# A two-layer decoder trunk on one core: the sums of the third modulation pair on VectorE

## The chip, the cores and the metric

The kernel runs on one core of a Trainium2 chip. Its engines work side by side, each through its own queue in order: TensorE (matrix products and transposes into PSUM; PE, with its weight loads as PEld), VectorE (DVE), ScalarE (ACT), GpSimd (POOL) and SyncE (SP), whose queue here issues nearly all large transfers. The metric is the device time of one execution in microseconds.

## The reference, cut to what matters

Two layers. In each, a conditioning vector `c` gives six modulation vectors of 1024 numbers. They shift, scale and gate the two halves of the layer:

```python
cond = jax.nn.silu(c)
mod = cond @ w_mod[l] + b_mod[l]            # w_mod[l]: 1024 x 6144
sh1, sc1, ga1, sh2, sc2, ga2 = split(mod, 6)
h = rms_norm(x, g_norm1[l]) * (1.0 + sc1) + sh1
z = h @ w_in[l]                             # 512 x 1024 by 1024 x 2560
... three token mixers on the parts of z, joined as y ...
x = x + ga1 * (y @ w_out[l])
h = rms_norm(x, g_norm2[l]) * (1.0 + sc2) + sh2
x = x + ga2 * hier_moe(h, ...)              # top-1 group, top-2 of 8 experts
```

All of it is float32. The six vectors are handled as three pairs of 2048 columns of `w_mod`: pair 0 is (sh1, sc1), pair 1 is (ga1, sh2), pair 2 is (sc2, ga2). Pair 2, "the third pair", is first used by the router's preparation (sc2) and by the experts (ga2).

## The kernel before, in words

Memory is an arena of 25 units of 128 x 2048 float32 (1 MiB each). `alloc` takes a free one, by default the one that has been free longest (`alloc(True)` the one freed last). All large weights go through one ordered stream: `want_layer` (L202) sorts the blocks of the input projection (`want_in`, two per chunk) and of pairs 1 and 2 (`want_mod`, eight each) by due step, `pump(keep)` issues blocks from SP as long as more than `keep` units are free, `get` hands one out and `release` frees it. SP is in program order, so a block whose unit is still being read holds up all blocks behind it. The order on the other engines in this stage is made by a planner that lists work by its own estimate of when it is ready.

The input projection of a layer runs as five chunks of 512 columns (`CHUNKS`: keys, queries, queries and keys of the third mixer, values, the rest), each of eight steps j, 40 steps in all (`z_chunk`, L486). A step contracts 128 rows for four tiles of 128 tokens. Each product is made of three (`mm3`, L301: high by high L302, high by low L303, low by high L304), so a step is twelve products of 128x512. The weights are split into a high half by ScalarE (L298) and a low half by GpSimd (L299), one split for every two steps, two buffers deep. After the eighth step the four accumulators (PSUM banks 0 to 3) are copied out, by ScalarE and VectorE in turn (L310, L308); the next chunk reuses the banks.

While a chunk is computed, the chunk before it is normalized and rotated (`rope_work`, L501): per token tile a square (ScalarE L506), a sum (VectorE L507), two small ScalarE steps (L294, L295), three products on VectorE (L512 twice at half width, L514), a sum on GpSimd (L516) and a product on VectorE (L518). TensorE transposes the four tiles at steps 4 to 7 (`heads_T`, L520; L523), and they are copied out again by L308 and L310. That is the work of chunks 1 to 3 beside the projection. Chunk 4 begins the softmax of the first mixer.

The modulation pairs 1 and 2 are computed in the same stage. A unit (`mod_unit`, L242, products at L245) takes one 128x2048 block of `w_mod` and makes four float32 products, side by side in four column tiles, with one column of silu(c), broadcast to 32, as weights; eight units sum in PSUM bank 7. `mods(c)` (L667) is called ahead of each step. With `PLAN[l] = (1, 18)` pair 1 has its units at steps 1, 3, ..., 15 and pair 2 at steps 18, 20, ..., 32. After the eighth, `mod_row` (L256) adds the bias, `mod_spread` (L272) writes the row to memory and reads it back as columns and as a broadcast, and `mod_finish` (L287) prepares the scale four steps later (`LATER`).

After the projection come the mixers, the output projection, the router, and the experts: 32 experts in 16 pairs per layer, with 6 MiB of weights each pair.

Of the kernel before, what the change touches and what calls it, by code (L numbers as in the profile page):

```python
# [18 lines left out]
OP = mybir.AluOpType  # L19
# [16 lines left out]

KA, QA, VA, QK, UV = 512, 0, 1024, 1792, 1536
CHUNKS = (KA, QA, QK, VA, UV)
PLAN = ((1, 18), (1, 18))
LEAD = (3, 3)  # L40
LATER = (4, 4)
ROOM = (0, 2)
# [36 lines left out]
def trunk(ctx: ExitStack, tc: tile.TileContext, I, out, dbg=None):  # L79
    nc = tc.nc  # L80
# [7 lines left out]
    PS = [psump.tile([128, 512], F32, name=f"ps{i}") for i in range(8)]  # L88
# [17 lines left out]
    def alloc(newest=False):  # L106
        return Unit(newest)
# [5 lines left out]
    ones_f = smallp.tile([128, 32], F32, name="ones_f")  # L113
    tok = smallp.tile([128, 2 * NT], F32, name="tok")
    ccol = smallp.tile([128, 8], F32, name="ccol")
    csil = smallp.tile([128, 8], F32, name="csil")
# [35 lines left out]
    def issue():  # L152
        key, parts = stream.popleft()
        u = alloc()
        held[key] = u
        for view, src in parts:
            nc.sync.dma_start(view(u.ap), src)

    def pump(keep=0):
        while stream and len(freed) > keep:  # L160
            issue()

    def get(key):
        while key not in held:
            issue()
        return held[key].ap

    def release(key):
        held.pop(key).free()

    def want_mod(l, i, j0=0, j1=8):
        w = I["w_mod"][l].rearrange("(p j) n -> p j n", j=8)
        for j in range(j0, j1):
            want(("mod", l, i, j), lambda a: a, w[:, j, i * 2048:(i + 1) * 2048])
# [10 lines left out]
    def want_out(l):  # L185
        w = I["w_out"][l].rearrange("(k p) n -> p k n", p=128)
        for h in range(4):
            want(("out", l, h), lambda a: a.rearrange("p (k n) -> p k n", k=2), w[:, 2 * h:2 * h + 2, :])
# [13 lines left out]
    def want_layer(l):  # L202
        if l == 0:
            want_mod(0, 0)
        g1, g2 = PLAN[l]
        need = [(8 * n + 4 * h - 2 - LEAD[l], want_in, (l, c, h)) for n, c in enumerate(CHUNKS) for h in range(2)]
        need += [(g + 2 * j, want_mod, (l, i, j, j + 1)) for i, g in ((1, g1), (2, g2)) for j in range(8)]
        for _, f, args in sorted(need, key=lambda x: x[0]):
            f(*args)
        if l + 1 < L:  # L210
            want_mod(l + 1, 0)
        want_out(l)
        for pr in range(16):
            want_pair(l, pr)
# [8 lines left out]
    for l in range(L):  # L223
        want_layer(l)
# [17 lines left out]
    def mod_unit(l, i, j, bank):  # L242
        w = get(("mod", l, i, j))
        for g in range(4):
            nc.tensor.matmul(PS[bank][32 * g:32 * g + 32, :], csil[:, j:j + 1].to_broadcast([128, 32]), w[:, g * 512:(g + 1) * 512],  # L245
                             start=j == 0, stop=j == 7, tile_position=(0, 32 * g))
        release(("mod", l, i, j))

    def mod_bias(l, i, bm, q=None):
        nc.vector.memset(bm, 0.0)  # L250
# [4 lines left out]
    def mod_row(bank, bm):  # L255
        nc.vector.tensor_tensor(mrow, PS[bank], bm, op=OP.add)  # L256
# [15 lines left out]
    def mod_spread(i):  # L272

        row = mod_d[i:i + 1, :]
        nc.sync.dma_start(row.rearrange("o (g n) -> (o g) n", g=4), mrow[0:128:32, :])
        col = lambda h: row[:, D * h:D * h + D].rearrange("o (p j) -> (o p) j", j=8)
        if i == 0:
            nc.sync.dma_start(cols[:, SH1, :], col(0))
            nc.sync.dma_start(cols[:, 6, :], col(1))
        elif i == 1:  # L280
            nc.sync.dma_start(cols[:, SH2, :], col(1))
            nc.sync.dma_start(ga1_of[0], row[:, 0:D].to_broadcast([128, D]))
        else:
            nc.sync.dma_start(cols[:, 6, :], col(0))
            nc.sync.dma_start(ga2, row[:, D:2 * D].to_broadcast([128, D]))

    def mod_finish(i):  # L287
        if i == 0:
            scaled(SC1, cols[:, 6, :], G1)
        if i == 2:  # L290
            scaled(SC2, cols[:, 6, :], G2)
# [29 lines left out]
    def front(l):  # L321
# [13 lines left out]
        W = [wk[i // 4].ap[:, 512 * (i % 4):512 * (i % 4) + 512] for i in range(16)]  # L335
# [3 lines left out]
        rpu = alloc()  # L339
        tab = rpu.ap.rearrange("p (n a m d) -> p n a m d", n=4, a=2, m=NT)  # L340
        hu = [alloc() for _ in range(4)]
# [102 lines left out]
        keep = [ROOM[l]]  # L444
# [36 lines left out]
        keep[0] = 1  # L481
        pump(keep[0])

        unit = [0]

        def z_chunk(done, each=None):  # L486
# [178 lines left out]


        def mods(c):  # L667
            g1, g2 = PLAN[l]

            def f(j):  # L670
                for i, g in ((1, g1), (2, g2)):
                    k, odd = divmod(8 * c + j - g, 2)
                    if 0 <= k < 8 and not odd:
                        mod_unit(l, i, k, 7)
                        pump(keep[0])
                        if k == 7:
                            mod_row(7, W[11 + i])
                            mod_spread(i)
                    if 8 * c + j == g + 14 + LATER[l]:
                        mod_finish(i)  # L680
            return f

        def zr(c):
# [70 lines left out]
        z_chunk(uv_done, both(mods(4), early))  # L754
        for k in range(2 * NT):
            nc.sync.dma_start(y_d[l][128 * k:128 * k + 128, :], I["k_zero"])
        for u in (rpu, *hu):
            u.free()
        yau, ycu, ypu, rt = [alloc() for _ in range(2)], alloc(), alloc(), alloc()
        U["yah"], U["yal"] = (u.ap.rearrange("p (h t) -> p h t", h=4) for u in yau)  # L760
# [525 lines left out]
```

## Time and profile before

| | us |
|---|---|
| median of 3 runs | 1162.53 |
| lowest and highest | 1159.25, 1163.12 |
| the profiled execution | 1165.25 |
| its span in the trace | 1163.3 |

Busy time in the profiled execution: TensorE 1053.3 us, its weight loads 573.1, VectorE 568.8, ScalarE 356.8, GpSimd 299.3. The busy time of an engine is a share of the whole; what bounds a stage is read from that stage. A row of a timeline gives start, duration, engine, line, operation, output and input with sizes; in brackets the idle time of the engine in front of it and what ended that.

### The profile page before, as it was taken

The page shows a single profiled execution, that of the slowest core. Times are in us where ns is not written, and L with a number is a line of the kernel's source. Part 1 is how long each engine was busy: PE and PEld are TensorE (multiplying, and loading weights), DVE is VectorE, ACT ScalarE, POOL GpSimd, SP SyncE. Part 2 cuts the span into 40 slices and gives each one's busy share as a digit, 9 for nine tenths or more (in the row PEclk, how much of TensorE's full clock was granted, in tenths as well). Part 3 has the DMA queues.
Part 4 walks back from the last instruction along what each step waited for, and adds up shares of the span by engine and source line. Part 5 has one row for each costly group of instructions (what it writes and reads, how often), then busy time and mean ns, then how long its engine had stood idle before and what let it go on. Part 6 is the DMA issues. An engine that isn't in the chain of part 4 may idle for free. (4 is left out here: it accounts for less than half of the span.)

```text
span 1163.3 us, 14911 instructions
## 1 busy us (share of the span) xinstructions
PE 1053.3 (91%) x5120; PEld 573.1 (49%) x5120; DVE 568.8 (49%) x1293; ACT 356.8 (31%) x900; POOL 299.3 (26%) x262
## 2 busy tenths in 40 slices
PE   5999999999899989989769999999988988999885
PEld 1567766577533323333227676667764333333322
DVE  3577756778622222222294777577775221222227
ACT  2333345564311111111132333556633111111110
POOL 5655531002222221221044555210022211122100
PEclk9899999999899999999979999999999999999998
DMA  9966436726849999999996535540477999999993
GB/s 378 397 222 250 163 116 220 291 72 232 310 140 399 410 390 409 390 375 398 402 317 256 181 127 181 181 133 2 143 291 262 385 409 409 399 399 384 400 396 126
DMA packets 91194, 329.91 MB, mean 284 GB/s; under 512 B 19288, under 2 KB 23576, under 8 KB 76448
## 3 DMA queue, kind: packets, MB, share of 16 engines
q1 hardware_dynamic: 74992, 307.86, 69.4%
q0 software_dynamic: 15184, 18.03, 4.9%
q10 hardware_dynamic: 864, 2.17, 0.5%
q8 instruction: 73, 1.20, 0.4%
q14 instruction: 81, 0.66, 0.2%
HBM read 338.87 MB, written 30.97 MB: 318 GB/s over the span
## 5 line engine op out<-in xcount | busy, mean ns | idle before, releaser
L1117 PE MATMUL ps<-unit,unit 128*64 128x512 f32 x1120 | 272.1, 611 | 19.2 <-DMA unit<-w 16.9
L1117 PEld LDWEIGHTS ps<-unit,unit 128*64 128x64 f32 x1120 | 88.4, 140 | 191.7 <-issue 180.5
L302 PE MATMUL ps<-unit,unit 128*128 128x512 f32 x448 | 182.1, 412 | 0.4 <-ACT unit L298 0.4
L303 PE MATMUL ps<-unit,unit 128*128 128x512 f32 x448 | 177.2, 396 | 2.8 <-POOL unit L299 1.5
L304 PE MATMUL ps<-unit,unit 128*128 128x512 f32 x448 | 176.0, 395 | 0.5 <-DVE unit L299 0.5
L1137 PE MATMUL ps<-unit,unit 128*64 128x512 f32 x560 | 138.1, 615 | 16.4 <-PEq L1185 14.7
L1122 DVE SCALAR_TENSOR_TENSOR unit<-ps,slot_f,unit 128x256 f32<-128x256 f32 x35 | 16.9, 484 | 251.9 <-ACT unit L1121 251.9
L1086 POOL DMA_INDIRECT unit<-xn_d,slot_i x62 | 63.0, 1017 | 285.0 <-PE ps L1097 164.3
L1121 ACT ACTIVATE unit<-ps 128x256 f32<-128x256 f32 x35 | 13.5, 385 | 392.2 <-PE ps L1117 392.2
L299 POOL TENSOR_TENSOR unit<-unit,unit 128x1024 fp32r<-128x1024 f32 (+1 forms) x46 | 104.9, 2284 | 102.0 <-ACT unit L298 102.0
L298 ACT ACTIVATE unit<-unit 128x1024 fp32r<-128x1024 f32 (+1 forms) x92 | 88.0, 963 | 117.1 <-PE ps L304 65.6
L302 PEld LDWEIGHTS ps<-unit,unit 128*128 128x128 f32 x448 | 84.4, 189 | 36.0 <-issue 16.4
L303 PEld LDWEIGHTS ps<-unit,unit 128*128 128x128 f32 x448 | 84.8, 189 | 22.4 <-DVE unit L299 3.5
L304 PEld LDWEIGHTS ps<-unit,unit 128*128 128x128 f32 x448 | 84.1, 188 | 19.2 <-DVE unit L299 1.2
L1151 DVE TENSOR_TENSOR unit<-ps,unit 128x512 f32<-128x512 f32 x62 | 42.9, 692 | 84.6 <-PE ps L1137 84.6
L1137 PEld LDWEIGHTS ps<-unit,unit 128*64 128x64 f32 x560 | 35.8, 137 | 90.5 <-issue 80.5
L534 ACT ACTIVATE unit<-unit,sm 128x512 f32<-128x512 f32 (+3 forms) x96 | 53.3, 556 | 32.9 <-DVE sm L532 32.4
L310 ACT ACTIVATE unit<-ps 128x512 f32<-128x512 f32 (+3 forms) x84 | 40.8, 490 | 72.0 <-PE ps L304 22.9
L1106 DVE TENSOR_SCALAR unit<-ps,cols 128x128 f32<-128x128 f32 x132 | 45.1, 405 | 33.5 <-PE ps L1097 32.6
L1091 POOL DMA_INDIRECT y_d<-unit,slot_y x31 | 31.6, 1020 | 113.4 <-DVEq L1187 46.5
L299 DVE TENSOR_TENSOR unit<-unit,unit 128x1024 fp32r<-128x1024 f32 (+1 forms) x46 | 54.9, 1199 | 11.0 <-ACT unit L298 10.4
L308 DVE COPY unit<-ps 128x512 f32<-128x512 f32 (+3 forms) x80 | 43.9, 553 | 31.8 <-PE ps L523 12.3
(223 smaller groups left out, 1317.0 us busy)
## 6 DMA issues: line engine op xcount, KB each, us to landing
unit<-w SPq DMA_DIRECT2D x256, 512.0 KB
unit<-w SPq DMA_DIRECT2D x64, 1024.0 KB
unit<-w_mod SPq DMA_DIRECT2D x48, 1024.0 KB
unit<-w_in SPq DMA_DIRECT2D x16, 1024.0 KB
y_d<-k_zero SPq DMA_DIRECT2D x16, 512.0 KB
unit<-w_out SPq DMA_DIRECT2D x8, 1024.0 KB
unit<-y_d SPq DMA_DIRECT2D x16, 512.0 KB
unit<-w_in SPq DMA_DIRECT2D x8, 512.0 KB
```

The costliest lines, as they stand in the source:

```text
L298: nc.scalar.activation(hi.bitcast(F32R), src, AF.Copy)
L299: (eng or nc.gpsimd).tensor_tensor(lo.bitcast(F32R), src, hi, op=OP.subtract)
L302: nc.tensor.matmul(o, ahi.bitcast(F32R), bhi.bitcast(F32R), start=first, stop=False)
L303: nc.tensor.matmul(o, ahi.bitcast(F32R), blo.bitcast(F32R), start=False, stop=False)
L304: nc.tensor.matmul(o, alo.bitcast(F32R), bhi.bitcast(F32R), start=False, stop=last)
L308: nc.vector.tensor_copy(dst, src)
L534: nc.scalar.activation(dst[:, :n], dst[:, :n], AF.Exp, bias=mx, scale=-1.0, accum_out=z)
L1086: nc.gpsimd.indirect_dma_start(out=dst, out_offset=None, in_=xn_d, in_offset=bass.IndirectOffsetOnAxis(ap=idx, axis=0), bounds_check=S - 1 ...
L1106: nc.vector.tensor_scalar(dst[:, j, :], p, cols[:, SC2, j:j + 1], cols[:, SH2, j:j + 1], op0=OP.mult, op1=OP.add)
L1117: nc.tensor.matmul(ph[64 * r:64 * r + 64, :], xT[:, j, 64 * r:64 * r + 64], ws[:, j % 4], start=j == 0, stop=j == 7, tile_position=(0, 64 ...
L1137: nc.tensor.matmul(PS[banks[n]][64 * r:64 * r + 64, :], hidT[b][:, j, 64 * r:64 * r + 64], w2[r][:, j, n, :], start=j == 0, stop=j == 1, t ...
L1151: nc.vector.tensor_tensor(ys[b][:, cs], p, ga2[:, cs], op=OP.mult)
```

## The change

Pair 1 stays as it is. Pair 2's eight blocks no longer go through TensorE as they come. VectorE multiplies each block by its column of silu(c), as a scalar per partition, and adds it to a 128 x 2048 accumulator `acc` that takes one unit of the arena until the end of chunk 4. The steps are 2, 6, ..., 30. At step 33 TensorE sums `acc` over the partitions with four products against ones; the bias row, the spread and the finish (step 37) follow as before. The due steps in the stream change alike.

```diff
-PLAN = ((1, 18), (1, 18))
+PLAN = ((1, 2, 33), (1, 2, 33))
...
-        need += [(g + 2 * j, want_mod, (l, i, j, j + 1)) for i, g in ((1, g1), (2, g2)) for j in range(8)]
+        need += [(g + d * j, want_mod, (l, i, j, j + 1)) for i, g, d in ((1, g1, 2), (2, g2, 4)) for j in range(8)]
...
+    def mod_part(l, i, j, acc):
+
+        w = get(("mod", l, i, j))
+        if j == 0:
+            nc.vector.tensor_scalar(acc, w, csil[:, j:j + 1], None, op0=OP.mult)
+        else:
+            nc.vector.scalar_tensor_tensor(acc, w, csil[:, j:j + 1], acc, op0=OP.mult, op1=OP.add)
+        release(("mod", l, i, j))
+
+    def mod_sum(acc, bank):
+        for g in range(4):
+            nc.tensor.matmul(PS[bank][32 * g:32 * g + 32, :], ones_f[:, 0:32], acc[:, g * 512:(g + 1) * 512],
+                             start=True, stop=True, tile_position=(0, 32 * g))
...
         keep[0] = 1
         pump(keep[0])
 
+        acc = alloc(True)
...
             def f(j):
-                for i, g in ((1, g1), (2, g2)):
-                    k, odd = divmod(8 * c + j - g, 2)
-                    if 0 <= k < 8 and not odd:
-                        mod_unit(l, i, k, 7)
-                        pump(keep[0])
-                        if k == 7:
-                            mod_row(7, W[11 + i])
-                            mod_spread(i)
-                    if 8 * c + j == g + 14 + LATER[l]:
-                        mod_finish(i)
+                now = 8 * c + j
+                k, odd = divmod(now - g1, 2)
+                if 0 <= k < 8 and not odd:
+                    mod_unit(l, 1, k, 7)
+                    pump(keep[0])
+                    if k == 7:
+                        mod_row(7, W[12])
+                        mod_spread(1)
+                k, odd = divmod(now - g2, 4)
+                if 0 <= k < 8 and not odd:
+                    mod_part(l, 2, k, acc.ap)
+                    pump(keep[0])
+                if now == e2:
+                    mod_sum(acc.ap, 7)
+                    mod_row(7, W[13])
+                    mod_spread(2)
+                if now == e2 + LATER[l]:
+                    mod_finish(2)
...
-        for u in (rpu, *hu):
+        for u in (acc, rpu, *hu):
             u.free()
```

## Rows read from the trace of the kernel before

**Rows 1.** The page, part 1: busy time, share and instructions of each engine.
```profile
PE 1053.3 (91%) x5120; PEld 573.1 (49%) x5120; DVE 568.8 (49%) x1293; ACT 356.8 (31%) x900; POOL 299.3 (26%) x262
```
**Rows 2.** By stretch, layer 0's chunks and its experts: busy, clock, DMA share, GB/s.
```profile
36.40:66.10 29.70, 29.10 (x128) 19.33 (x129) 12.99 (x16) 10.00 (x15) 20.57 (x15) 0.91 1.02 393
66.10:95.60 29.50, 28.73 (x146) 19.93 (x145) 22.02 (x26) 10.46 (x21) 14.93 (x8) 1.00 0.60 220
95.60:122.80 27.20, 27.20 (x138) 19.72 (x136) 21.37 (x25) 10.58 (x21) 15.04 (x8) 1.00 0.44 152
122.80:151.00 28.20, 28.20 (x145) 19.93 (x144) 21.19 (x25) 9.87 (x22) 14.98 (x8) 1.00 0.54 187
400.00:592.00 192.00, 167.46 (x698) 62.04 (x696) 50.32 (x97) 26.88 (x82) 33.86 (x37) 0.96 1.01 388
```
**Rows 3.** The same view, layer 1's chunks 1 to 3.
```profile
640.00:668.50 28.50, 27.73 (x140) 19.02 (x139) 20.74 (x24) 10.44 (x20) 14.94 (x8) 1.00 0.51 182
668.50:696.00 27.50, 27.50 (x141) 20.14 (x141) 21.89 (x25) 10.54 (x20) 15.03 (x8) 1.00 0.40 137
696.00:725.00 29.00, 29.00 (x149) 20.47 (x148) 22.32 (x27) 10.39 (x21) 14.96 (x8) 1.00 0.54 182
```
**Rows 4.** TensorE's waits in layer 0's projection: total us, times, longest.
```profile
PE ps L303 <- POOL unit L299: 0.8, 1, 0.8
```
**Rows 5.** TensorE's timeline around two modulation units.
```profile
55.74 1.06 PE L245 MATMUL ps<-unit,csil 128*32 128x512 f32 x8
...
61.85 0.39 PE L303 MATMUL ps<-unit,unit 128*128 128x512 f32 x1
62.08 0.39 PE L304 MATMUL ps<-unit,unit 128*128 128x512 f32 x1
62.40 1.06 PE L245 MATMUL ps<-unit,csil 128*32 128x512 f32 x8
63.40 0.50 PE L302 MATMUL ps<-unit,unit 128*128 128x512 f32 x1
```
**Rows 6.** VectorE's groups by form, whole span: total us, mean ns, idle before.
```profile
L1207 DVE TENSOR_TENSOR unit<-unit,unit 128x1024 f32<-128x1024 f32 x16 | 18.9, 1220 | 11.7 <-DMA unit<-y_d 11.6
L567 DVE SCALAR_TENSOR_TENSOR unit<-unit,sm 128x512 f32<-128x512 f32 x8 | 6.0, 752 | 0.3
L567 DVE SCALAR_TENSOR_TENSOR unit<-unit,sm 128x128 f32<-128x128 f32 x8 | 2.8, 352 | 0.2
L641 DVE TENSOR_SCALAR unit<-unit,sm 128x512 f32<-128x512 f32 x8 | 3.8, 487 | 0.0
L641 DVE TENSOR_SCALAR unit<-unit,sm 128x128 f32<-128x128 f32 x8 | 2.1, 284 | 0.1
```
**Rows 7.** VectorE's timeline in chunk 0: its longest idle times.
```profile
55.83 0.15 DVE L393 TENSOR_SCALAR gsub<-gsub 128x1 f32<-128x1 f32 x1 [6.45 <-DMA gsub<-g_sub_a]
65.03 0.43 DVE L512 TENSOR_TENSOR unit<-unit,unit 128x256 f32<-128x256 f32 x1 [9.05 <-ACT unit L310]
```
**Rows 8.** VectorE's timeline in chunk 2.
```profile
96.62 0.75 DVE L512 TENSOR_TENSOR unit<-unit,unit 128x256 f32<-128x256 f32 x2
97.28 2.88 DVE L514 TENSOR_TENSOR unit<-unit,unit 128x512 f32<-128x512 f32 x1
...
101.74 0.68 DVE L518 TENSOR_TENSOR unit<-unit,sm 128x512 f32<-128x512 f32 x1
102.34 0.68 DVE L514 TENSOR_TENSOR unit<-unit,unit 128x512 f32<-128x512 f32 x1
102.94 0.67 DVE L507 TENSOR_REDUCE sm<-unit 128x8 f32<-128x512 f32 x1
...
105.27 2.95 DVE L512 TENSOR_TENSOR unit<-unit,unit 128x256 f32<-128x256 f32 x2
...
113.08 2.86 DVE L518 TENSOR_TENSOR unit<-unit,sm 128x512 f32<-128x512 f32 x1 [1.40 <-ACT unit L310]
115.86 0.68 DVE L308 COPY unit<-ps 128x512 f32<-128x512 f32 x1
```
**Rows 9.** GpSimd's timeline in chunk 2: the splits.
```profile
97.12 2.50 POOL L299 TENSOR_TENSOR unit<-unit,unit 128x1024 fp32r<-128x1024 f32 x1 [4.84 <-ACT unit L298]
...
105.31 2.62 POOL L299 TENSOR_TENSOR unit<-unit,unit 128x1024 fp32r<-128x1024 f32 x1 [0.85 <-ACT unit L298]
...
113.01 2.38 POOL L299 TENSOR_TENSOR unit<-unit,unit 128x1024 fp32r<-128x1024 f32 x1
```
**Rows 10.** GpSimd's groups in chunk 2 (95.6 to 122.8 us).
```profile
L299 POOL TENSOR_TENSOR unit<-unit,unit 128x1024 fp32r<-128x1024 f32 x4 | 9.9, 2476 | 7.0 <-ACT unit L298 7.0
L516 POOL TENSOR_TENSOR unit<-unit,unit 128x512 f32<-128x512 f32 x4 | 5.2, 1293 | 4.8 <-DVE unit L514 4.8
```
**Rows 11.** TensorE's timeline in chunk 2: units and transposes.
```profile
107.91 1.06 PE L245 MATMUL ps<-unit,csil 128*32 128x512 f32 x8
108.91 0.66 PE L523 MATMUL ps<-ident,unit 128*128 128x128 f32 x4
...
119.70 0.60 PE L523 MATMUL ps<-ident,unit 128*128 128x128 f32 x4
```
**Rows 12.** ScalarE's timeline in chunk 2, around a conversion of weights.
```profile
102.45 0.30 ACT L294 ACTIVATE sm<-sm,eps_t 128x8 f32<-128x8 f32 x1 [1.02 <-DVE unit L518]
...
104.19 1.05 ACT L298 ACTIVATE unit<-unit 128x1024 fp32r<-128x1024 f32 x1
```
**Rows 13.** The third pair's finish on VectorE, step 34's first products, the finish's first reader.
```profile
159.92 0.17 DVE L259 SCALAR_TENSOR_TENSOR cols<-cols 128x8 f32<-128x8 f32 x1
160.40 1.13 PE L543 MATMUL ps<-unit,unit 64*128 64x512 f32 x4
L914 DVE TENSOR_TENSOR unit<-unit,cols x2: 173/180/186, 192.7 to 770.7; 128x32 f32<-128x32 f32 x2
```
**Rows 14.** SP's timeline: issues of pair 1's blocks of steps 3 to 9.
```profile
27.54 2.96 SPq L157 DMA_DIRECT2D unit<-w_mod  x2
...
35.75 1.82 SPq L157 DMA_DIRECT2D unit<-w_mod  x2
```
**Rows 15.** GpSimd's splits, whole span: shortest, median and longest in ns.
```profile
L299 POOL TENSOR_TENSOR unit<-unit,unit x46: 1289/2392/2815, 37.3 to 746.1; 128x1024 fp32r<-128x1024 f32 x38, 128x512 fp32r<-128x512 f32 x8
```

More of the change, by code (lines that the diff above doesn't have):

```diff
@@ L204, in want_layer @@
             want_mod(0, 0)
-        g1, g2 = PLAN[l]
+        g1, g2, _ = PLAN[l]
         need = [(8 * n + 4 * h - 2 - LEAD[l], want_in, (l, c, h)) for n, c in enumerate(CHUNKS) for h in range(2)]
-        need += [(g + 2 * j, want_mod, (l, i, j, j + 1)) for i, g in ((1, g1), (2, g2)) for j in range(8)]
+        need += [(g + d * j, want_mod, (l, i, j, j + 1)) for i, g, d in ((1, g1, 2), (2, g2, 4)) for j in range(8)]
         for _, f, args in sorted(need, key=lambda x: x[0]):
@@ L667, in mods @@
         def mods(c):
-            g1, g2 = PLAN[l]
+            g1, g2, e2 = PLAN[l]
             def f(j):
-                for i, g in ((1, g1), (2, g2)):
-                    k, odd = divmod(8 * c + j - g, 2)
-                    if 0 <= k < 8 and not odd:
-                        mod_unit(l, i, k, 7)
-                        pump(keep[0])
-                        if k == 7:
-                            mod_row(7, W[11 + i])
-                            mod_spread(i)
-                    if 8 * c + j == g + 14 + LATER[l]:
-                        mod_finish(i)
+                now = 8 * c + j
[16 more added lines that the diff above has]
+                    mod_finish(2)
             return f
```

## The prediction

> **What bounds the kernel now.** I read the page first: TensorE is busy 91% of the span, VectorE 49%, GpSimd 26% [rows 1]. These are averages, so I went to the stage that the change touches, the input projection: per layer 40 steps in five chunks of eight, of which chunks 0 to 3 matter here. In layer 0 the turns of the chunks lie at about 36, 66.1, 95.6, 122.8 and 151.0 us; layer 1 repeats the picture some 575 us later. In the table by stretch TensorE is busy for all of chunks 2 and 3 and for all but 0.8 us of chunk 1, in both layers, at full clock [rows 2, 3]. The list of TensorE's waits has a single 0.8 us on GpSimd's low half of the weights [rows 4]. So TensorE sets the pace there, and what leaves its queue is worth its pitch, until something else is late. The rest of the text asks what is late next.
>
> **TensorE: what goes.** A modulation unit is four column-tiled products. The product before one starts at 62.08 us, the first after it at 63.40: 1.32 us, where two ordinary products stand 0.23 apart [rows 5]. A unit costs 1.09 us. Per layer eight go (those at steps 18, 20, ..., 32) and one like them comes (the sum over partitions, at step 33). Net seven: 7 x 1.09 = 7.6 us per layer, 15.3 us for both. By place: three before the end of chunk 2 (3.3 us), four before the end of chunk 3 (4.4 us), none in chunk 1; in chunk 4 one leaves and one comes. Were it all, 1165.3 us of the profiled execution would become 1150.0, and the median 1162.5 (2.7 us below that execution) would become 1147.3.
>
> **VectorE: what comes.** No row shows its 128x2048 operation with two inputs in SBUF; the nearest bound it. The same form takes 0.752 us for 512 columns and 0.352 for 128, 1.04 ns per column, so 2.35 us for 2048; 1024 columns of a plain sum take 1.22, twice that is 2.44 [rows 6]. I take 2.35, or 2.3 from start to start. The first step of a layer has one input; 0.487 and 0.284 us at 512 and 128 columns give 1.30 [rows 6]. Per layer 1.3 + 7 x 2.35 = 17.8 us. The steps fall at 2 and 6 of every chunk from 0 to 3: two per chunk.
>
> **Where that lands.** In chunk 0 VectorE is idle for long: 6.45 and 9.05 us in front of two of its instructions [rows 7]. Two steps are free there. Chunks 1 to 3 are another matter. They hold the rope work: per chunk VectorE runs some twenty operations, GpSimd four splits and four sums, and the two disturb each other. A 128x512 product that takes 0.68 us alone takes 2.88 when GpSimd starts a split at about the same time (97.28 against 97.12); the same at 105.27 and 113.08 against 105.31 and 113.01 [rows 8, 9]. So a VectorE operation with two inputs in SBUF stands still for a GpSimd operation, and their times add. The new step is of this kind. The load of chunk 2:
> - GpSimd: 9.9 us of splits and 5.2 of sums, 15.1 us [rows 10].
> - VectorE, undisturbed, start to start: eight half-width operations at 0.34 and eight full ones at 0.60 us, 7.5 us [rows 8].
> - Together 22.6 us which exclude each other. The old length is 27.2; TensorE alone would need 27.2 - 3.3 = 23.9.
> - With two new steps 22.6 + 4.6 = 27.2 us. With one, 24.9.
>
> That is the heart of the forecast: with two steps in a chunk this pair of engines needs as long as the chunk takes today. It is no loose bound, since from the chunk's start to the last rope operation (115.94 us) the pair already works almost without a gap. Chunk 3 is 28.2 us now, its load the same. Something is lost at each turn, where VectorE must first empty the accumulators; I take 0.7 us, below the 0.8 of rows 4 and above nothing.
>
> **Who waits for VectorE.** TensorE transposes the roped tiles at steps 4 to 7. The last at step 7 starts at 119.70, its operand is done at 115.94: 3.8 us of slack, of which the removed units take 3.3 [rows 8, 11]. The accumulators are copied by VectorE too, behind whatever is queued. And ScalarE's conversion of the next weights (104.19) stands in its queue behind a rope instruction that waits for VectorE, so the split behind it ends at 107.93, and its first reader stands some 1 us later [rows 9, 11, 12]. A new step before these places pushes all three.
>
> **Order on VectorE.** It is the planner's, not the program's: the finishing of the third pair, written at step 36, ran at 159.92 us, when TensorE was only about to begin step 34 (160.40) [rows 13]. So a new step may run as soon as its block is in and a gap is planned. The arena lets blocks come some six steps ahead in chunk 1; I expect about one step per layer to move from the later chunks forward to idle time in chunk 0 or at the end of chunk 1, and cannot tell more from the trace.
>
> **The sum, likeliest case, per layer.** Chunk 1: unchanged but for one more wait of the size of rows 4, +0.8. Chunk 2 with two steps: 27.2 + 0.7 = 27.9 against 27.2, +0.7. Chunk 3 with one: 24.9 + 0.7 = 25.6 against 28.2, -2.6. Total -1.1, for two layers -2.2 us: 1163.0 for the profiled execution, 1160.3 on the footing of the median. No part of the 15.3 us is lost on TensorE; it is handed to the other two engines.
>
> **DMA and queues.** The same 48 blocks, each 1 MiB, come in another order: two of the third pair stand ahead of needed ones in chunk 0, where DMA is full at 393 GB/s: 2 x 2.7 = 5.3 us later for the second pair's. Their units at steps 5 and later came from blocks issued 25 us and more before use [rows 5, 14], so I price this at nothing; if that cover were gone it would be up to 5.3 us, once. In chunks 1 to 3 DMA is busy 0.44 to 0.60, which covers one buffer less. SP now waits for VectorE before it reuses a third-pair buffer, with the input weights queued behind; at 137 to 220 GB/s that has room [rows 2, 3]. A new step waits for its block on VectorE, and behind it wait rope work and copies: the blocks come early enough except for that same 5.3. The bias row, the spread and the finish move one step later (2.7 us); the first reader of the result runs 33 us after the finish [rows 13], so nothing. The experts' stage is bound by DMA at 388 GB/s [rows 2], but its stream begins when buffers come free, which moves with the front, so I let gains and losses through in full.
>
> **A rule against the change.** The splits stretch little: 2.39 us in the median, 2.82 at most [rows 15], so by the rows VectorE holds GpSimd up by 0.4 us at most. The Trainium skill (SBUF — State Buffer, Who interferes with whom) says that whichever of the two starts first holds the shared port for its whole instruction and the other blocks fully. No operation of 2.3 us on VectorE meets a split in this trace, so it shows only the one side. By the rows, the sum above stands; by the rule, a split meeting a new step ends up to 2.3 us late, and the split behind which TensorE stands is already just in time. That is the slow rival below.
>
> **Rivals.**
> 1. **Splits held (slower).** A new step starts just ahead of a split and holds it; TensorE stands for it, and the roped tiles come late. For it: the chain of rows 8, 9 and 12 has 1 us of slack. Against: the planner may put steps elsewhere. Per layer: chunk 1 one step on the chain, +2.35; chunk 2 the rope ends 20.3 + 4.7 = 25.0 us in, then a transpose (0.44) and a step (2.73), 28.2, +1.0; chunk 3 the same 28.2, 0. Together +3.4, two layers +7: 1169.3. With a further 2.35 in chunks 2 and 3 it is +16, 1178. It decides when both steps of a chunk run before its last rope operation.
> 2. **More hoisting (faster).** Two steps or more leave chunks 2 and 3 for idle time. Chunks 2 and 3 at 25.6 each: -1.6 - 2.6 = -4.2 per layer, -8.4: 1154.1.
> 3. **All hidden.** The full 15.3 us: 1147.3. Against it: 23.9 us for TensorE is less than 24.9 for the pair with even one step.
> 4. **The order undone.** The planner bunches steps late, ahead of the softmax of chunk 4: about rival 1's time, and counted there.
>
> **How the numbers follow.** A measurement can tell about 0.3%, 3.5 us, from no change. Chances: likeliest (1159 to 1166) 0.40; rival 1 0.27; rival 2 0.25; rival 3 0.08. Faster is 2 and 3, 0.33; same 0.40; slower 0.27. The range goes from 1150, which leaves out rival 3 and a corner of 2, to 1174, which leaves out the upper half of rival 1; together under 0.2. The likeliest case's own range is 1157 to 1166.
>
> **What would show it.** Right: 16 of 48 units gone from TensorE (eight records each, so 128 of 384) and two new sums over partitions, 16 new VectorE operations of 2.3 us, some stretched by GpSimd; chunk 2 as long as before and chunk 3 shorter; new idle time of TensorE on GpSimd's split, on VectorE's rope results and on its copies, of several us per layer. Wrong: TensorE gapless with chunks 2 and 3 under 25 us (rivals 2, 3), or splits later by 2 us with chunk 1 longer by over 2 (rival 1), or new steps waiting for DMA.

## The result and the profile after

The changed kernel takes 1178.17 us in the median of four runs (1175.88 to 1178.80), the kernel before 1162.82 beside it. The ratio is 1.0124 with a 95% interval of 1.0098 to 1.0149: slower by 14.4 us, above the top of the range (1174). The profiled execution is the fastest of the four, 1175.88 us with a span of 1174.0, against 1165.25 and 1163.3. One execution on record, the profiled one of e1 below, was far slower than all others of its kernel (5101.77 us) and enters no figure.

The page, part 1, answers [rows 1]: TensorE lost 11.3 us of busy time, VectorE gained 43.8.

```profile
PE 1042.0 (89%) x5008; PEld 576.6 (49%) x5008; DVE 612.6 (52%) x1309; ACT 355.7 (30%) x900; POOL 314.1 (27%) x262
```

The new operation, all its records in both layers (shortest, median, longest in ns, first and last start):

```profile
L255 DVE SCALAR_TENSOR_TENSOR unit<-unit,csil,unit x14: 2337/2344/4477, 56.9 to 725.5; 128x2048 f32<-128x2048 f32 x14
```

By stretch, from turn to turn (a turn is ScalarE's first rope square of the next chunk; the last stretch ends at the first softmax operation); columns as in [rows 2]. First layer 0's chunks 1, 2 and 3, then layer 1's:

```profile
64.49:94.03 29.54, 28.78 (x146) 19.89 (x145) 25.89 (x27) 10.43 (x21) 17.43 (x8) 1.00 0.68 254
94.03:124.78 30.75, 27.18 (x122) 20.51 (x121) 27.98 (x28) 10.20 (x21) 15.40 (x8) 0.94 0.55 195
124.78:160.69 35.91, 28.69 (x124) 22.38 (x122) 27.41 (x30) 12.14 (x24) 16.96 (x8) 0.90 0.26 88
647.51:677.08 29.57, 28.65 (x146) 19.91 (x145) 27.65 (x27) 10.53 (x21) 17.66 (x8) 1.00 0.57 213
677.08:708.38 31.30, 26.41 (x114) 20.39 (x113) 25.29 (x27) 10.32 (x20) 17.02 (x8) 0.95 0.38 131
708.38:741.53 33.15, 28.18 (x124) 21.98 (x122) 25.14 (x29) 12.14 (x24) 16.95 (x8) 0.95 0.29 96
```

With the same ends the kernel before has 29.45, 27.18 and 31.84 us in both layers, at a clock of 1.00. So chunk 1 is unchanged, chunk 2 grew by 3.6 and 4.1 us, chunk 3 by 4.1 and 1.3: 13.1 us, nearly the whole loss. TensorE has seven units fewer in these two stretches of layer 0 and eight fewer in layer 1 (in layer 0 pair 1's last unit came later and fell into chunk 2, at 95.59 us): 15 x 1.09 = 16.4 us less to do. So some 29.5 us of new delay came in.

TensorE's waits (total us, times, longest) in layer 0's projection, which answer [rows 4], then in layer 1's:

```profile
PE ps L538 <- DVE unit L322: 7.8, 2, 6.7
PE ps L317 <- POOL unit L313: 2.8, 3, 1.5
...
PE ps L538 <- DVE unit L322: 5.5, 2, 4.4
...
PE ps L317 <- POOL unit L313: 3.4, 3, 1.9
PE ps L316 <- DVE unit L322: 1.9, 1, 1.9
```

L538 is the transpose of a roped tile, L322 VectorE's copy out of PSUM, L313 the split. Where the single wait was 0.8 us, waits from turn to softmax are now 3.6 + 7.2 us in layer 0's chunks 2 and 3 and 4.9 + 5.0 in layer 1's (length less TensorE's busy time). About 9 us more are in no list of waits. Most of it is the clock: in each of these four stretches TensorE did some 3 to 4.5 us of its work at half clock, 14.5 us in all by the granted clock in slices of 1 us. Half of that is lost, an estimated 7 us.

How it comes about is seen in chunk 2 of layer 0. VectorE's timeline, the counterpart of [rows 8]:

```profile
109.96 2.34 DVE L255 SCALAR_TENSOR_TENSOR unit<-unit,csil,unit 128x2048 f32<-128x2048 f32 x1
112.23 0.68 DVE L533 TENSOR_TENSOR unit<-unit,sm 128x512 f32<-128x512 f32 x1
...
114.89 2.82 DVE L533 TENSOR_TENSOR unit<-unit,sm 128x512 f32<-128x512 f32 x1 [1.38 <-POOL unit L531]
117.64 4.46 DVE L255 SCALAR_TENSOR_TENSOR unit<-unit,csil,unit 128x2048 f32<-128x2048 f32 x1
122.02 0.68 DVE L322 COPY unit<-ps 128x512 f32<-128x512 f32 x1
```

ScalarE, GpSimd and TensorE in the same stretch:

```profile
112.94 0.30 ACT L308 ACTIVATE sm<-sm,eps_t 128x8 f32<-128x8 f32 x1 [7.46 <-DVE unit L533]
113.15 1.04 ACT L312 ACTIVATE unit<-unit 128x1024 fp32r<-128x1024 f32 x1
...
114.81 5.14 POOL L313 TENSOR_TENSOR unit<-unit,unit 128x1024 fp32r<-128x1024 f32 x2
...
114.82 0.66 PE L538 MATMUL ps<-ident,unit 128*128 128x128 f32 x4 [0.89 <-ACT unit L324]
115.23 0.47 PE L316 MATMUL ps<-unit,unit 128*128 128x512 f32 x1
117.22 0.50 PE L317 MATMUL ps<-unit,unit 128*128 128x512 f32 x1 [1.51 <-POOL unit L313]
...
118.53 0.63 PE L318 MATMUL ps<-unit,unit 128*128 128x512 f32 x1
118.96 0.63 PE L316 MATMUL ps<-unit,unit 128*128 128x512 f32 x1
...
122.76 0.66 PE L538 MATMUL ps<-ident,unit 128*128 128x128 f32 x4 [1.17 <-DVE unit L322]
```

Read it in two chains. The first step, at 109.96, pushes the rope product at 112.23. ScalarE waits for that product, and the conversion of the next weights stands in its queue behind it (113.15); the split follows at 114.81, where it was 113.01 in [rows 9], and TensorE stands 1.51 us for it. The second step, at 117.64, begins beside a running split and takes 4.46 us. Behind it stands the copy of tile 1 out of a PSUM bank (122.02, where [rows 8] has 115.86), and tile 3's transpose needs that bank: 122.76, where [rows 11] has 119.70. From 118.1 to about 121.2 products follow one another in 0.43 us, not 0.23: TensorE's second level, 1.2 GHz.

Chunk 3 of layer 0 has the same two chains, and the longer wait. VectorE, GpSimd and TensorE:

```profile
141.88 2.34 DVE L255 SCALAR_TENSOR_TENSOR unit<-unit,csil,unit 128x2048 f32<-128x2048 f32 x1
145.37 2.81 DVE L533 TENSOR_TENSOR unit<-unit,sm 128x512 f32<-128x512 f32 x1 [1.15 <-POOL unit L531]
148.11 2.34 DVE L255 SCALAR_TENSOR_TENSOR unit<-unit,csil,unit 128x2048 f32<-128x2048 f32 x1
150.37 0.74 DVE L322 COPY unit<-ps 128x256 f32<-128x256 f32 x2
...
142.03 3.30 POOL L531 TENSOR_TENSOR unit<-unit,unit 128x512 f32<-128x512 f32 x1 [1.57 <-DVE unit L529]
145.30 2.33 POOL L313 TENSOR_TENSOR unit<-unit,unit 128x1024 fp32r<-128x1024 f32 x1
...
136.89 0.60 PE L538 MATMUL ps<-ident,unit 128*128 128x128 f32 x4
...
150.93 1.09 PE L538 MATMUL ps<-ident,unit 128*128 128x128 f32 x4 [6.68 <-DVE unit L322]
```

The first step holds GpSimd's rope sum (3.30 us; before, all 24 of these sums took 1.29 to 1.31). The last rope product then waits, and is itself stretched by the split that begins beside it; the second step goes ahead of the copies. Tile 0 was transposed at 136.89 and could have been copied from 137.5 on; its copy by VectorE runs at 150.37, and the third transpose of the chunk, tile 2's, which uses tile 0's bank, waits 6.68 us for it.

Chunk 2 of layer 1 went another way. There both steps, at 678.94 and 696.32, run ahead of the last rope product (702.81). The second one holds a split, and TensorE stands for that split. VectorE, GpSimd and TensorE:

```profile
696.32 2.35 DVE L255 SCALAR_TENSOR_TENSOR unit<-unit,csil,unit 128x2048 f32<-128x2048 f32 x1
...
697.67 3.20 POOL L313 TENSOR_TENSOR unit<-unit,unit 128x1024 fp32r<-128x1024 f32 x1 [2.33 <-ACT unit L312]
...
700.92 0.50 PE L317 MATMUL ps<-unit,unit 128*128 128x512 f32 x1 [1.90 <-POOL unit L313]
```

### The profile page after: what moved, and what is told of

It reads as the page before. It is cut to its first block, busy times and chain, and to the rows that moved or that the text cites. A ratio compares the mean times of both kernels' runs of the same rounds, so it can differ in the third digit from the quotient of the medians.

```text
span 1174.0 us, 14726 instructions
## 1 busy us (share of the span) xinstructions
PE 1042.0 (89%) x5008; PEld 576.6 (49%) x5008; DVE 612.6 (52%) x1309; ACT 355.7 (30%) x900; POOL 314.1 (27%) x262
## 5 line engine op out<-in xcount | busy, mean ns | idle before, releaser
L317 PE MATMUL ps<-unit,unit 128*128 128x512 f32 x448 | 180.9, 404 | 7.4 <-POOL unit L313 6.2
L316 PE MATMUL ps<-unit,unit 128*128 128x512 f32 x448 | 184.3, 417 | 2.6 <-DVE unit L322 1.9
L318 PE MATMUL ps<-unit,unit 128*128 128x512 f32 x448 | 178.3, 401 | 0.5 <-DVE unit L313 0.5
L313 POOL TENSOR_TENSOR unit<-unit,unit 128x1024 fp32r<-128x1024 f32 (+1 forms) x46 | 110.8, 2414 | 93.5 <-ACT unit L312 93.5
L316 PEld LDWEIGHTS ps<-unit,unit 128*128 128x128 f32 x448 | 86.1, 193 | 33.8 <-issue 14.6
L317 PEld LDWEIGHTS ps<-unit,unit 128*128 128x128 f32 x448 | 86.2, 193 | 31.5 <-POOL unit L313 8.3
L318 PEld LDWEIGHTS ps<-unit,unit 128*128 128x128 f32 x448 | 85.8, 192 | 19.6 <-DVE unit L313 1.2
L1160 PEld LDWEIGHTS ps<-unit,unit 128*64 128x64 f32 x560 | 35.3, 136 | 88.4 <-issue 56.4
L322 DVE COPY unit<-ps 128x512 f32<-128x512 f32 (+3 forms) x80 | 43.7, 552 | 34.4 <-PE ps L538 10.3
L313 DVE TENSOR_TENSOR unit<-unit,unit 128x1024 fp32r<-128x1024 f32 (+1 forms) x46 | 53.1, 1160 | 10.7 <-ACT unit L312 10.1
## 6 DMA issues: line engine op xcount, KB each, us to landing
unit<-w SPq DMA_DIRECT2D x256, 512.0 KB, 13.3
y_d<-k_zero SPq DMA_DIRECT2D x16, 512.0 KB, 11.6
```

Of the source, the lines that this page charges most:

```text
L313: (eng or nc.gpsimd).tensor_tensor(lo.bitcast(F32R), src, hi, op=OP.subtract)
L316: nc.tensor.matmul(o, ahi.bitcast(F32R), bhi.bitcast(F32R), start=first, stop=False)
L317: nc.tensor.matmul(o, ahi.bitcast(F32R), blo.bitcast(F32R), start=False, stop=False)
L318: nc.tensor.matmul(o, alo.bitcast(F32R), bhi.bitcast(F32R), start=False, stop=last)
L322: nc.vector.tensor_copy(dst, src)
L1160: nc.tensor.matmul(PS[banks[n]][64 * r:64 * r + 64, :], hidT[b][:, j, 64 * r:64 * r + 64], w2[r][:, j, n, :], start=j == 0, stop=j == 1, t ...
```

## The experiments

The table gives, for every kernel but e1, the time from chunk 1's first turn to the first softmax in each layer, read from the timelines of its profiled execution, and the ratio of its time to that of the kernel before, measured beside it.

| kernel | layer 0, us | layer 1, us | time, ratio [95%] |
|---|---|---|---|
| before | 88.5 | 88.5 | 1 |
| after | 96.2 | 94.0 | 1.0124 [1.0098, 1.0149] |
| e2_half_columns | 92.4 | 90.1 | 1.0038 [1.0017, 1.0058] |
| e3_tiles_by_scalar | 88.9 | 91.7 | 1.0003 [0.9982, 1.0024] |
| e4_units_back | 92.8 | 94.9 | 1.0072 [1.0051, 1.0093] |
| e5_before_tiles_by_scalar | 88.4 | 88.4 | 0.9967 [0.9952, 0.9981] |
| e6_all_copies_by_scalar | 93.8 | 85.5 | 1.0007 [0.9991, 1.0024] |
| e7_one_input | 85.3 | 84.3 | 1.0028 [1.0008, 1.0048] |
| e8_four_and_four | 86.4 | 85.3 | 1.0022 [1.0005, 1.0038] |
| e9_one_column_again | 85.2 | 86.1 | 0.994, one run |
| e10_before_no_units | 86.3 | 84.7 | 0.9943 [0.9921, 0.9964] |
| e11_four_and_four_tiles | 85.3 | 84.1 | 0.9939 [0.9920, 0.9957] |
| e12_own_bank | 93.4 | 93.5 | 1.0102 [1.0068, 1.0136] |
| e13_banks_apart | 89.5 | 93.6 | 1.0056 [1.0033, 1.0079] |
| e14_before_banks_apart | 88.5 | 88.5 | 0.9998 [0.9978, 1.0019] |

**Is it VectorE's time? e1 and e2.** The seven adding steps work on one column, or on half.

```diff
-            nc.vector.scalar_tensor_tensor(acc, w, csil[:, j:j + 1], acc, op0=OP.mult, op1=OP.add)
+            nc.vector.scalar_tensor_tensor(acc[:, 0:1], w[:, 0:1], csil[:, j:j + 1], acc[:, 0:1], op0=OP.mult, op1=OP.add)
```

> Changed kernel, but the seven adding steps of a layer work on 1 of 2048 columns (the rest of pair 2's sums is left out); blocks, buffers, order and TensorE's work stay. Theory V (the time of the steps on VectorE makes the change slow): the median falls from 1178 to 1150-1157 us, below the kernel before, as 7.6 us per layer leave TensorE and only part of it is caught by the rope work. Rival S (the other order of the stream and the arena's missing unit make it slow): it stays at 1170 or more.

> The same with 1024 of 2048 columns, about 1.27 us a step in place of 2.34 (half of pair 2's sums left out). Theory V: some 14 x 1.07 = 15 us of VectorE time less, of which most counts: 1162-1168 us. Rival S: 1170 or more. If only whole collisions with GpSimd count, and not length, it stays above 1172 too.

e1 took 1157.98 us, 0.9935 [0.9913, 0.9958]. Its trace is read from one more execution of the same kernel, e9.

> The kernel with one column per adding step once more, for its trace (seven steps' sums of pair 2 left out). Theory V: in each layer the stretch from the first chunk turn to the first softmax is 5-7 us shorter than before (88.5 us there), with TensorE's waits in it under 2 us, and two thirds or more of what both layers gain reaches the end. If the rope work alone held TensorE, the waits for splits would be 3 us or more in a layer and the gain under 4 us.

2048, 1024 and 1 column give 1.0124, 1.0038 and 0.9935: the length of the step is the cause, not that it exists, and not the new order of the blocks, which all three have. It also bounds what the removal could ever bring. Nearly all of VectorE's new work is gone in e9, and 5.7 us of the 15.3 reach the softmax (1157.98 against 1165.11 at the end); still standing are TensorE's waits, 4.9 us for copies and 4.8 for splits in the whole span:

```profile
PE ps L538 <- DVE unit L322: 4.9, 2, 2.4
PE ps L317 <- POOL unit L313: 4.8, 7, 0.9
```

**Is TensorE still the bound? e4.** Seven dummy units per layer go back to TensorE at steps 18 to 30, on another bank.

```diff
+                if now in range(18, 32, 2):
+                    for g in range(4):
+                        nc.tensor.matmul(PS[4][32 * g:32 * g + 32, :], csil[:, g:g + 1].to_broadcast([128, 32]), hT[g],
+                                         start=True, stop=True, tile_position=(0, 32 * g))
```

> Changed kernel with seven dummy units per layer put back on TensorE at steps 18 to 30 (four products of 512 columns each from data at hand, result unused), so TensorE has the work of the kernel before and VectorE that of the changed one. If TensorE still sets the pace in chunks 2 and 3 the 15.3 us come on top: 1190-1194. If the other engines set it, the units fall into TensorE's waits: 1178-1184.

1174.16 us, 1.0072: fourteen units more and no longer than the changed kernel. In chunks 2 and 3 TensorE is not the bound any more; the removed work left idle time, not a shorter chunk. Chunk 2 of layer 0 is 30.78 us with the units (clock 1.00) and 30.75 without (0.94). In layer 1 VectorE runs the same operations in the same order in both kernels: 94.9 us with seven units more, 94.0 without. In layer 0 the order differs in places, so the 6 us by which the ratios favour e4 are not read. One thing goes with them: with the units the granted clock stays at 1.00 in three of the four stretches (0.95 in chunk 2 of layer 1), where it fell in all four without.

**The copies: e3, with its control e5.** The copies of the transposed tiles go to ScalarE, in the changed kernel and in the kernel before.

```diff
-                copy(m + k, d[:, :, 128 * m:128 * m + 128],
+                copy(0, d[:, :, 128 * m:128 * m + 128],
```

> Changed kernel with the copies of the transposed tiles all on ScalarE, in place of every second one on VectorE behind the new step. Theory Q (the cost is TensorE's wait for those copies, 13.4 us in its list of waits): that wait falls under 2 us, and the time to 1164-1169 us. Rival C (VectorE's rope work is as late as the copies): the wait moves to the tiles' operands or the accumulators, and the time stays at 1173-1178.

> Control: the kernel before with the copies of the transposed tiles all on ScalarE. Theory Q (those copies cost only where a new step stands ahead of them): no change against the kernel before, within 3 us. Rival G (ScalarE is the better engine for them in any case): faster by 8 us or more, as the changed kernel was.

e3 is at 1.0003: the loss is gone. But the control gains too (0.9967), with its projection unchanged at 88.4 us; where those 3.8 us come from I did not find. Against the control the changed kernel still loses 0.4%. By this pair, the copies behind the steps are some two thirds of the loss.

**All copies: e6.** The accumulators' copies of these chunks go to ScalarE too.

```diff
-            z_chunk(lambda m: copy(m, z[m], PS[m]), each)
+            z_chunk(lambda m: copy(0, z[m], PS[m]), each)
```

> Changed kernel with the copies of the transposed tiles and those of the accumulators of chunks 0 to 2 all on ScalarE. If accumulators still wait behind new steps, 2-4 us come off the variant with only the tiles on ScalarE: 0.2-0.3% under the kernel before. If what is left is GpSimd's held splits (10.4 us in that variant's list of TensorE's waits), no change against it, level with the kernel before; ScalarE's fuller queue could make it 2-4 us slower.

1.0007, no better than e3. Layer 1 gained 6 us on it (85.5), layer 0 lost 5 (93.8): in layer 0 TensorE's waits for the split became 10.0 us, since ScalarE's conversion now stands behind the copies. The queue that one unloads fills another that TensorE waits for.

**Does the step exclude GpSimd? e7.** e3 with the adding step replaced by a sum of the block along its row: one input from SBUF, of the same length.

```diff
-            nc.vector.scalar_tensor_tensor(acc, w, csil[:, j:j + 1], acc, op0=OP.mult, op1=OP.add)
+            nc.vector.tensor_reduce(acc[:, j:j + 1], w, axis=mybir.AxisListType.X, op=OP.add)
```

> The variant with the tiles on ScalarE, with each of the seven adding steps replaced by a sum along the row of the same block (one SBUF input, about the same 2.2 us; pair 2's sums are left out). Theory E (exclusion: a step with two SBUF inputs and a split on GpSimd stand still for each other): the new operations are no longer stretched, TensorE's 10 us of waits for splits fall under 4 us, and the time is 4-8 us below the kernel before. Rival O (mere occupancy of VectorE): time and waits as in the variant with the tiles on ScalarE, level with the kernel before.

VectorE's second step of chunk 2, beside a split, in e3's timeline and then in e7's:

```profile
117.72 4.46 DVE L255 SCALAR_TENSOR_TENSOR unit<-unit,csil,unit 128x2048 f32<-128x2048 f32 x1
```
```profile
118.24 2.27 DVE L255 TENSOR_REDUCE unit<-unit 128x1 f32<-128x2048 f32 x1
```

GpSimd's rope sums from 64 to 165 us (groups by form: total us, mean ns, idle before), in e3 and then in e7:

```profile
L531 POOL TENSOR_TENSOR unit<-unit,unit 128x512 f32<-128x512 f32 x12 | 19.6, 1632 | 17.6 <-DVE unit L529 17.6
```
```profile
L531 POOL TENSOR_TENSOR unit<-unit,unit 128x512 f32<-128x512 f32 x12 | 15.5, 1290 | 17.6 <-DVE unit L529 17.6
```

With the row sum the two engines do not touch; with two inputs, whichever began later stands. The projection is 3.6 and 7.4 us shorter than in e3, so the exclusion is worth that much there. The total does not follow (1.0028); more on this below.

**Half of it: e8 and e11.** Steps 2, 6, 10 and 14 stay on VectorE, the other four units go back to TensorE at steps 18, 22, 26 and 30 and sum into one bank with `mod_sum`. e11 also has e3's copies.

```diff
-                    mod_part(l, 2, k, acc.ap)
+                    if k < 4:
+                        mod_part(l, 2, k, acc.ap)
+                    else:
+                        mod_unit(l, 2, k, 7, 4, -1)
```

> Changed kernel with only the first four steps of pair 2 on VectorE (2, 6, 10, 14: chunks 0 and 1) and the other four as units on TensorE at steps 18, 22, 26, 30, summed in the same bank. Net three units per layer off TensorE, 3 x 1.09 x 2 = 6.5 us. If chunks 2 and 3 are where the steps do harm, and chunk 1 hides two: 4-6.5 us below the kernel before (0.35-0.55%). If steps in chunk 1 cost as much as those in chunks 2 and 3: level or up to 4 us slower.

> Four steps on VectorE in chunks 0 and 1, four units on TensorE, and the copies of the transposed tiles on ScalarE. By the runs so far the projection of a layer should be 3 us shorter than before in each layer. If that reaches the end: 0.995 of the kernel before or less. If the layer's turn and the experts' stage give it back as in the variant without ScalarE's copies: 0.998 to 1.002.

In both the projection is shorter, by 5.3 and 7.5 us over both layers. In e11 it shows as time: 1156.88 us, 0.9939 [0.9920, 0.9957], below both kernels. By stretch, e11's chunks 2 and 3 of layer 0: TensorE is busy for all of it, at full clock.

```profile
95.13:122.39 27.26, 27.26 (x138) 19.81 (x137) 17.98 (x23) 11.62 (x22) 15.59 (x8) 1.00 0.58 219
122.39:150.91 28.52, 28.52 (x140) 20.95 (x138) 21.46 (x25) 13.46 (x28) 15.31 (x8) 1.00 0.34 111
```

The steps lie in chunks 0 and 1, where chunk 1 absorbs its two at no cost (also in the changed kernel), and three units per layer, net, are gone from TensorE: 6.5 us, about what the projections are shorter. At the end it is less clear. How much of e11's time is the steps' and how much e5's copies is not told apart by more than the 3 us between 0.9967 and 0.9939, whose intervals touch; and e8, with the same steps and the old copies, is no faster than the kernel before (1.0022).

**TensorE's units alone: e10.** The kernel before, seven of the third pair's units per layer cut to one column.

```diff
+        n = 1 if i == 2 and j else 512
-            nc.tensor.matmul(PS[bank][32 * g:32 * g + 32, :], csil[:, j:j + 1].to_broadcast([128, 32]), w[:, g * 512:(g + 1) * 512],
+            nc.tensor.matmul(PS[bank][32 * g:32 * g + 32, 0:n], csil[:, j:j + 1].to_broadcast([128, 32]), w[:, g * 512:g * 512 + n],
```

> The kernel before with seven of pair 2's eight units per layer cut to one column per product (their sums are left out): TensorE's saving without any work for VectorE, at the old places in the stream. If TensorE's saving reaches the end in full: 15 us, 0.987 of the kernel before. If the rope work holds TensorE for part of it, or the experts' stage, which is bound by DMA, gives part of it back: 6-10 us, about 0.993, as the one-column kernel had.

1155.64 us, 0.9943. A cut unit still takes some 0.25 us, so about 0.83 goes with each (chunk 2, with two of them, is 25.52 us for 27.18): 11.6 us in all. 6.0 reach the softmax. The largest part of the rest is a new wait, twice 2.0 us, for the same copy, with nothing new on VectorE:

```profile
PE ps L524 <- DVE unit L309: 4.0, 2, 2.0
```

So the copy was next in line in the kernel before already. In its chunk 3 VectorE copies tiles 0 and 1 one behind the other, and tile 2's transpose needs tile 0's bank:

```profile
143.12 0.74 DVE L308 COPY unit<-ps 128x256 f32<-128x256 f32 x2
...
144.80 0.66 PE L523 MATMUL ps<-ident,unit 128*128 128x128 f32 x4
```

The first of the two copies ends at 143.53, so it had 1.3 us of slack. The four cut units of this chunk ahead of that transpose take 4 x 0.83 = 3.3 us from it, and the 2.0 us between are the wait.

**Which bank: e12, e13 and the control e14.** e12 gives tile 3's transposes a bank of their own. e13 gives tile 2 its own and puts tile 3 in tile 0's, so that no tile shares with the one two before it; e14 does that in the kernel before. The copies stay where they were, and VectorE's order is the changed kernel's.

```diff
-            pb = PS[5 + m % 2]
+            pb = PS[(5, 6, 5, 4)[m]]
```
```diff
-            pb = PS[5 + m % 2]
+            pb = PS[(5, 6, 4, 5)[m]]
```

> Changed kernel; only the fourth transposed tile gets an accumulator bank of its own, so that TensorE need not wait for the copy of the second one; all copies stay on VectorE behind the new steps. Theory Q in its narrow form (the shared bank is what TensorE waits for): the 13 us of waits of the transposes go, the time is as with the copies on ScalarE, level with the kernel before. Rival A (the next thing in VectorE's queue, the accumulators' copies, takes its place): waits of the first products of a chunk for VectorE's copies grow to 4-8 us, and the time stays at 1.006 or more.

> The changed kernel with tile 2's transposes in a PSUM bank of their own and tile 3's in the bank of tile 0, so that no transpose shares a bank with the tile two before it; the copies stay on VectorE, behind the same steps in the same order. If TensorE's long waits for copies are for that shared bank (theory), the 13.4 us of transposes waiting for copies fall below 3, the granted clock of chunk 3 returns from 0.90 to about 1, chunk 2 of layer 0 goes from 30.75 to some 28 us and chunk 3 to its softmax from 35.9 to 28 to 31, and the time to 1158 to 1166 (0.995 to 1.003 of the kernel before), some of the gain given back in the experts. If the copies are needed late in any case (rival: the roped tiles, the accumulators and the splits wait for the same steps), the waits only change their name and the time stays at 1172 to 1180.

> Control: the kernel before with the same banks. It has no wait of the transposes for copies in its projection, so theory and rival both expect no change: 0.997 to 1.003.

e12 changed little (1.0102), which seems to end the bank theory. But in chunk 2 of layer 0, where tile 3 had waited for tile 1's copy, that wait is gone (27.8 us for 30.75, the clock at 1.00 for 0.94); the 6.7 us in chunk 3 stand, because there it is tile 2 that waits for tile 0. e13 takes both away: 1.0056, half the loss, and the control shows that the banks by themselves are worth nothing (0.9998). e13's waits of TensorE in layer 0's projection, then in layer 1's:

```profile
PE ps L317 <- POOL unit L313: 6.6, 4, 2.8
...
PE ps L538 <- DVE unit L322: 0.3, 1, 0.3
...
PE ps L317 <- POOL unit L313: 4.9, 4, 2.8
PE ps L316 <- DVE unit L322: 2.2, 1, 2.2
PE ps L538 <- DVE unit L533: 2.1, 1, 2.1
```

Both theories had a part. The transposes' waits for copies fall from 13.3 to 0.3 us, and half the loss with them; but waits for splits, for roped tiles and for the accumulators' copies, all three behind the same steps, grow from 8.1 to 15.8 us and keep the other half, and the clock falls after them (0.90 in chunk 2 of layer 1, 0.94 in chunk 3). In the projection all of the gain lies in layer 0 (6.7 us; 0.4 in layer 1). The time, 1169.61, lies above the 1166 that I gave the bank theory and below its rival's 1172.

## Why the prediction was wrong, and where it was right

**Right: the prices.** The new step takes 2.34 us alone, where 2.35 was taken from [rows 6]; the first step 1.28 in layer 1 and 2.31 beside a split in layer 0. A unit's records fell from 384 to 256, with sixteen records of sums new. In layer 0 no adding step waited for its block.

**Half right: what is late next.** "Who waits for VectorE" named the roped tiles, the accumulators' copies and the split behind ScalarE's conversion. The split became a wait in both layers (6.2 us in all) and the accumulators' copies in one place (1.9 us). For a roped tile TensorE waits only once the copies are out of the way (2.1 us in e13). The largest wait, 13.3 us, was not on the list: the copy of an earlier tile out of the bank that the next transpose needs. "All hidden" was rightly given little, but not for its reason, that the pair is longer than TensorE with even one step: e10 has no step at all, and half of its 11.6 us is lost all the same, most of it to that copy.

**Wrong: the price of being late.** This is the step that failed. "Where that lands" made a chunk as long as the load of VectorE and GpSimd (22.6 + 4.6 = 27.2 us), plus 0.7 at the turn. The load was no larger than that: the time in which one of the two is at such an operation is 26.0 us in chunk 2 of both layers, 21.8 before. The chunks took 30.8 and 31.3. So a chunk is not its load: TensorE needs splits and copies at fixed places in its own queue, and the loads are late in bursts. "The sum" has +0.7 for chunk 2 and -2.6 for chunk 3; measured are +3.6 and +4.1 in layer 0, +4.1 and +1.3 in layer 1. The slack was read for the last rope operation only: 3.8 us, of which the removed units take 3.3. The copy of a transposed tile out of the bank it shares, which stands behind the second step, is in no term of the sum; "behind whatever is queued" speaks of the accumulators. Its slack could be read: in [rows 8, 11] tile 1's copy ends at 116.54 and tile 3's transpose starts at 119.70, 3.2 us, which three removed units take up; in chunk 3 it was 1.3. e10 shows that none is left once the units are gone, and e13 that these copies are half of the loss.

**Wrong: the clock.** The sum lets TensorE run at full clock, as in [rows 2, 3]. After the new waits, or during the longest, the granted clock fell to 0.50 in chunks 2 and 3 of both layers, for 3 to 4.5 us of TensorE's work each time. Of the 29.5 us of delay, 20.7 are waits; the rest is mostly this. TensorE's busy time in chunk 2 of layer 0 hides it: 27.18 us before and after, with two units fewer (122 records for 138).

**Half right: the order.** One step was to move forward from chunk 3 to idle time. In layer 1 it did (seven adding steps start at 630.0, 640.2, 665.5, 672.4, 678.9, 696.3 and 725.5, one of them in chunk 3), in layer 0 none. But layer 1's single step at 725.48 held the rope sum (3.31 us) and led to a wait of 4.4 us all the same, so the 2.6 us that it was to bring did not come.

**The rule against the change.** Whichever of the two engines starts first holds the other for the whole instruction, as the Trainium skill says (SBUF — State Buffer, Who interferes with whom): now both sides show. A split holds a step (4.46 for 2.34 us), a step holds a rope sum (3.30 for 1.29), and steps hold splits in layer 1: the longest takes 3.81 us, where the longest before took 2.82 [rows 15]. The same section of the Trainium skill says that an operation with at most one SBUF input does not contend, outside VectorE's two-port modes, and that its reduction never does. e7 agrees for the reduction: its steps are 2.27 to 2.29 us, all fourteen. The first step of a layer, a product with one SBUF input, does contend: at 49.97 us, beside a split, it takes 2.31 us for 1.28. Whether it ran in a two-port mode no run shows.

**Rival 1** had the sign, and its upper end, 1178, is the time measured. Its mechanism is what happened in one of the four chunks, chunk 2 of layer 1: there both steps came ahead of the last rope operation, its deciding point, and the second held a split. In layer 0 splits were seldom held (2515 ns in the mean from 64 to 165 us, before 2459); they were late because ScalarE's conversion stood behind a late rope operation, and the transposes were late for a copy, since the second step came behind the last rope operation and ahead of the copies. The time agrees with its upper half by chance as much as by cause; cutting that half from the range was the error there.

**The experts.** "I let gains and losses through in full" stood up. Changes in the projection and in the total agree within 4 us for after (+13.3 and +14.4), e2, e3, e4, e6, e9 to e14 and the control e5. e7 and e8 are the exceptions: 7.3 and 5.3 us shorter in the projection, 3.3 and 2.6 us longer in the total. What ate these 8 to 11 us is open. Two things are seen. From the experts' first product to the next layer's first transposes e7 takes 295.0 us, e8 291.5, before 289.7. And from those transposes to the first turn of layer 1's chunk 1 they take 36.1 and 36.3 us, before 32.6; but e11 and the control e14 take 36.1 too, without such a loss.

**DMA.** Priced at nothing for lack of a conflict; layer 1 shows one. A step of chunk 0 waits 5.74 us for its block (640.19) and costs nothing. Another waits 1.50 us at 678.94, the accumulators' copies stand behind it, and TensorE waits 1.88 us at 681.94. The prediction named that queue and no price.

## What to carry to other kernels

Work moved to an engine with idle time is priced by its place, not by the load: list what stands in that engine's queue behind each new operation, and give each item its slack against the engine that sets the pace, the copy that frees a buffer no less than the one that fills it. Two buffers used in turn are a deadline for the copy of the one before last; where long operations come in between, a third buffer, or a copy on another queue, is worth trying first. Move only as many pieces as the chunks with real slack can take: four of eight steps made the projections 5.3 us shorter (e8), eight made them 13.3 us longer.

## What the runs showed of the hardware

TensorE's granted clock fell to half after short waits in a stretch where it was otherwise busy: in chunk 2 of layer 0 after waits of 0.89 and 1.51 us, within 1 us of the end of the second (118.1 us), and it was back at about 121.2. It stayed for the 0.8 us of [rows 4], and in e12 it stayed at 1.00 in the same chunk after waits of 0.89 and 1.52. In e10 a wait of 2.0 us brought it down in layer 0 and one of the same length in layer 1 did not. So waits of this size put the clock at risk, not more; what decides is open.

A short operation of VectorE can pay for a long one of GpSimd and the other way round, and the cost can travel: in chunk 3 a step held a rope sum for 2.0 us, and the rope product behind it was so moved into the next split, where it took 2.81 us for 0.68.
